# Gated attention with both heads of a pair in one 128-row operand

## Chip, cores and metric

One core of one Trainium2 chip. The metric is the device time of one execution in microseconds (us); runs of a kernel are compared by their median.

## What is computed

One layer of a decoder on 1024 tokens of width 1024, in float32. Only the two parts that the change touches are shown whole; `h` is the normalized input times `w_in`, cut into column groups.

```python
# group A: gated linear attention, 4 heads, dk = 64, dv = 128, low-rank gate of 16 columns
log_a = log_sigmoid(glr @ w_alpha2 + b_alpha) / 16
b     = cumsum(log_a) within a chunk;  qe = q * exp(b);  ke = k * exp(-b)
A     = where(causal, qe @ ke.T, 0)
o     = A @ v + qe @ S_prev              # S: the running 64 x 128 state of a head
S     = S * exp(b_last) + (k * exp(b_last - b)).T @ v
o     = rms_norm(o) * silu(gr)
# group B: sliding-window softmax attention, 8 query heads on 2 key heads of 64
...
x = x + concat(o_A, o_B) @ w_out
x = x + (silu(a) * b) @ w_down           # [a, b] = causal_conv3(rms_norm(x) @ w_up)
```

The kernel takes 128 tokens at a time (8 tiles of tokens, `t` = 0 to 7), not chunks of 64: `b` is counted from the middle of the 128, so that the same formulas hold for them.

## The kernel before

The program is a list of small steps, each put down with a due time by `at(time, step, ...)`, sorted by it and issued in that order. The due times are in units of one dense block of the projection (24 matmuls). `TQ, TK, TV, TG, TR, TO = 0.0, 8.0, 12.8, 20.8, 28.8, 36.8` are the starts of the stages: query projection of group B, its keys with the low-rank gate, values of group A, its queries and keys, its output gate, and the output projection; after that come the two large matrix products of the MLP (`product` and `down_pair`). The container in which the program is built then orders each engine's instructions by a planner with a timeline of its own, so that a step's instructions can stand inside a dense block that the list has ahead of it or behind it; buffers and dependences hold either way.

Large products are split into a high and a low float32r part and take three passes each (`PASSES`); the small products of the gated attention are plain float32 and show as two records of a matmul and two weight loads each in the trace.

The steps around the change, for a tile `t`:

- `kvl_post`, `kvl_tr`, `kvl_la` (due at TK + 0.6 t, + 1.9 and + 3.1): the 16 gate columns and a column of ones are transposed into 17 rows of a PSUM bank (L352), ACT copies them to `gt` (L362, one buffer), and the matmul L368 multiplies these 17 rows by `wa`, 16 rows of `w_alpha2` and one of `b_alpha`. ACT and DVE turn the result `za` into `la`.
- `gla_exp` (L457 to L482): running sums of `la` by matmuls with a triangle (`bd`), exponentials on ACT, and the decays `dec`.
- `gla_qk`, `gla_tr`: queries and keys are scaled from the bank of the dense block and transposed, four transposes into one bank (L498). One ACT copy (L500) takes the bank to `gqt`: two column blocks of queries, two of keys, each with the two heads of a pair in rows 0 to 63 and 64 to 127.
- `gla_state`: `cs`, the state's update, by four matmuls of 64 columns (L508), added to `state` on DVE. `gla_mid` (L523): ACT scales the four heads of the state, 64 rows each, into the two diagonal blocks of `s_mid`, whose other blocks stay zero.
- `gla_a` (due at TG + t + 1.9): the scores `ga`. For each half of the rows (`lo`) two matmuls that contract over 64 rows (L532), in a bank of their own, and a masked copy (L534, DVE) into `asb`.
- `gla_o` (due at TG + t + 2.7): four matmuls of the scores with the values (L543), and, but for the first tile, two with 256 columns of queries against the diagonal `s_mid` (L546), in the same bank. ACT and DVE then take squares, sums and a copy.
- `gate` and `gate_tr`: output gate and transposes `ogt` for the output projection.

Beside these run the steps of group B (`swa_qt`, `swa_scores`, `swa_pt`, `swa_pv`: tiles `qpt`, `sc`, `ppt`, `pv`) and the dense blocks `dk`, `dv`, `dg`, `dr`, `do` (L283, 24 matmuls each).

Banks of PSUM come from two pools of four, taken in turn (`bank`). `k2_tile` takes one of four buffers of 128 x 512.

Of the kernel before, what the change touches and what calls it, by code (L numbers as in the profile page):

```python
# [9 lines left out]
F32 = mybir.dt.float32  # L10
F32R = mybir.dt.float32r
I32 = mybir.dt.int32
AF = mybir.ActivationFunctionType
# [4 lines left out]
P = 128  # L18
# [12 lines left out]
HALF = (slice(0, 64), slice(64, 128))  # L31
# [3 lines left out]
def hymba_layer_kernel(ctx, tc, x, mix_norm, w_in, w_alpha2, b_alpha, gla_norm,  # L35
# [3 lines left out]
    act, dve, pool, pe, sp = nc.scalar, nc.vector, nc.gpsimd, nc.tensor, nc.sync  # L39
# [15 lines left out]
    def bank(name):  # L55
        ps["n"] += 1
        if "f" in ps:
            return ps["f"][2 + ps["n"] % 2]

        for start, which in (("n2pt_6", "b"), ("do1_7", "a"), ("n2pt_3", "a")):  # L60
            if name.startswith(start):
                return ps[which].tile([P, 512], F32, tag="b", name=name)
        return ps["ab"[ps["n"] % 2]].tile([P, 512], F32, tag="b", name=name)
# [40 lines left out]
    gl = sg.enter_context(tc.tile_pool(name="gl", bufs=1))  # L104
# [10 lines left out]
    amask = gl.tile([P, P], I32, name="amask")  # L115
# [40 lines left out]
    def rms_scale(ss, n, w, name, p, tag, bufs=3):  # L156
        v = p.tile([P, w], F32, tag=tag + "v", name=name + "v", bufs=bufs)
        dve.tensor_scalar(v, ss, 1.0 / n, EPS, op0=ALU.mult, op1=ALU.add)
        r = p.tile([P, w], F32, tag=tag + "r", name=name + "r", bufs=bufs)
        pool.tensor_tensor(r, v, mhalf[:, :w], ALU.pow)  # L160
        return r
# [128 lines left out]
    kt = gl.tile([P, 2, T + P], F32R, name="kt")  # L290
# [4 lines left out]
    sinks_s = gl.tile([P, 8], F32, name="sinks_s")  # L295
    qkn = gl.tile([P, 2], F32, name="qkn")
    wqk = gl.tile([P, 1], F32, name="wqk")
    wa = gl.tile([17, 256], F32, name="wa")
    glan = gl.tile([P, 1], F32, name="glan")

    def load_small():
# [10 lines left out]
    def k2_tile(name):  # L312
        return gl.tile([P, 512], F32, tag="k2", name=name, bufs=K2)
# [19 lines left out]
    kvl = {}  # L333
# [14 lines left out]
    def kvl_tr(t):  # L348
        kn, gn = kvl[t]
        pt = bank(f"kpt{t}")  # L350
        pe.transpose(pt[:, 0:P], kn, ident)
        pe.transpose(pt[0:17, P:2 * P], gn, ident)  # L352
        c = (t + 1) * P
        kl = gl.tile([P, P], F32R, tag="kl", name=f"kl{t}", bufs=2)
        for g in range(2):
            r, o = HALF[g], HALF[1 - g]
            act.activation(kt[r, g, c:c + P], pt[r, 0:P], AF.Copy, scale=wqk[r])
            dve.scalar_tensor_tensor(kl[r], pt[r, 0:P], wqk[r], kt[r, g, c:c + P].bitcast(F32),
                                     op0=ALU.mult, op1=ALU.subtract)
            act.dma_start(kt[o, g, c:c + P].bitcast(F32), kl[r].bitcast(F32))  # L360
        gt = gl.tile([17, P], F32, tag="gt", name=f"gt{t}", bufs=1)
        act.copy(gt, pt[0:17, P:2 * P])  # L362
        kvl[t] = gt

    def kvl_la(t):
        gt = kvl[t]
        pt = bank(f"za{t}")
        pe.matmul(pt[:, 0:256], lhsT=gt, rhs=wa, start=True, stop=True)  # L368
        z = pt[:, 0:256]
        e = k2_tile(f"lae{t}")[:, 0:256]  # L370
        act.activation(e, z, AF.Abs)
        act.activation(e, e, AF.Exp, scale=-1.0)
        act.activation(e, e, AF.Ln, bias=1.0)
        dve.scalar_tensor_tensor(la[:, t, :], z, 0.0, e, op0=ALU.min, op1=ALU.subtract)
# [72 lines left out]

    state = gl.tile([P, 2, P], F32, name="state")  # L450
    s_mid = [gl.tile([P, 2, 256], F32, name=f"s_mid{i}") for i in range(2)]
    asb = [gl.tile([P, 2, 256], F32, name="asb0")]
    for s in s_mid + asb:
        pool.memset(s, 0.0)
    gkd, gdec, gex, gqk, gqt, glh, grs, vg = {}, {}, {}, {}, {}, {}, {}, [None]

# [37 lines left out]
    def gla_tr(t):  # L494
        qk = gqk[t]
        pb = bank(f"gt{t}")
        for i in range(4):
            pe.transpose(pb[:, i * P:(i + 1) * P], qk[:, i * P:(i + 1) * P], ident)  # L498
        qt = k2_tile(f"gqt{t}").rearrange("p (i c) -> p i c", i=4)
        act.copy(qt, pb.rearrange("p (i c) -> p i c", i=4))  # L500
        gqt[t] = qt

    def gla_state(t):
        kd, v, dc = gkd[t], vg[0][:, t, :], gdec[t]
# [12 lines left out]

    def gla_mid(t):
        dc, sm = gdec[t], s_mid[t % 2]
        for h in range(4):  # L520
            pr, lo = h // 2, h % 2
            r = HALF[lo]
            act.activation(sm[r, pr, lo * P:(lo + 1) * P], state[r, pr], AF.Copy,  # L523
                           scale=dc[r, pr * 2:pr * 2 + 1])

    def gla_a(t):
        qt = gqt[t]
        for lo in range(2):
            pb = bank(f"ga{t}_{lo}")
            r = slice(lo * 64, (lo + 1) * 64)  # L530
            for pr in range(2):
                pe.matmul(pb[:, pr * P:(pr + 1) * P], lhsT=qt[r, 2 + pr, :], rhs=qt[r, pr, :],  # L532
                          start=True, stop=True)
            dve.copy_predicated(asb[0][:, lo].rearrange("p (q c) -> p q c", q=2),  # L534
                                amask.rearrange("p (q c) -> p q c", q=1).broadcast_to((P, 2, P)),
                                pb[:, 0:256].rearrange("p (q c) -> p q c", q=2))

    def gla_o(t):
        qt, a, v = gqt[t], asb[0], vg[0][:, t, :]
        pb = bank(f"go{t}")  # L540
        for h in range(4):
            pr, lo = h // 2, h % 2
            pe.matmul(pb[:, h * P:(h + 1) * P], lhsT=a[:, lo, pr * P:(pr + 1) * P],  # L543
                      rhs=v[:, h * P:(h + 1) * P], start=(h == 0), stop=(t == 0 and h == 3))
        for pr in range(2 if t else 0):
            pe.matmul(pb[:, pr * 256:(pr + 1) * 256], lhsT=qt[:, pr, :], rhs=s_mid[t % 2][:, pr, :],  # L546
                      start=False, stop=(pr == 1))
        sq = k2_tile(f"gsq{t}")
        act.activation(sq, pb, AF.Square)
        ss = gl.tile([P, 4], F32, tag="gss", name=f"gss{t}", bufs=2)  # L550
        dve.tensor_reduce(ss, sq.rearrange("p (h d) -> p h d", d=P), op=ALU.add, axis=AX.X)
        dve.tensor_copy(v, pb)
        grs[t] = rms_scale(ss, P, 4, f"g{t}", gl, "gr", 8)
# [438 lines left out]
    def at(time, f, *a):  # L992
        ev.append((time, len(ev), f, a))
# [7 lines left out]
    for c in halves:  # L1001
        pb = bank(f"mix{len(mix_ps)}")
# [7 lines left out]
    TQ, TK, TV, TG, TR, TO = 0.0, 8.0, 12.8, 20.8, 28.8, 36.8  # L1010
# [23 lines left out]
    for t in range(NT):  # L1034
        if t > 1:
            if t > 2:
                at(t - 2.7, load_x, t)
                at(t - 2.5, norm1_stat, t)
            if t > 2:
                at(t - 1.6, norm1_tr, t)  # L1040
            at(TQ + t, unit_q, t)
        at(TK + 0.6 * t, unit_k, t)
        at(TK + 0.6 * t + 1.9, kvl_tr, t)
        at(TK + 0.6 * t + 3.1, kvl_la, t)
        at(TV + t, unit_v, t)
        at(TG + t, unit_g, t)
        at(TR + t, unit_r, t)
        at(TO + t, unit_o, t, 0)
        u = TO + 8 + (2 * t if t < 4 else 2 * t - 7)
        at(u, unit_o, t, 1)  # L1050
        at(u + 0.005, norm2_rows, t)
        if t < 7:
            at(u + 1.9, norm2_tr, t)
        if 4 <= t < 7:
            at(u + SUMS, norm2_sums, t)
# [15 lines left out]
    for t in range(NT):  # L1071
        s = 11.0 + 1.9 * t
        at(s - 0.3, swa_qt, t)
        at(s + 1.0, swa_scores, t, 0)
        at(s + 1.6, swa_scores, t, 1)
        at(s + 3.2, swa_pt, t, 0)
        at(s + 3.8, swa_pt, t, 1)
        at(s + 4.9, swa_pv, t)
        s = TG + t
        at(s - 2.4, gla_lh, t)  # L1080
        at(s - 1.4, gla_exp, t)
        at(s + 1.0, gla_tr, t)
        if t < NT - 1:
            at(s + 1.8, gla_state, t)
            at(s + 1.85, gla_mid, t + 1)
        at(s + 1.9, gla_a, t)
        at(s + 2.7, gla_o, t)
        at(TR + t + 1.3, lambda tt=t: gate_tr(tt, psb.pop(("r", tt))))
# [113 lines left out]
```

## Time and profile before

| | |
|---|---|
| median of 3 runs | 1078.79 us (1077.31 to 1079.29) |
| profiled execution | 1077.32 us, span 1075.5 us |
| TensorE (PE) busy | 1061.8 us, 99% |
| weight loads (PEld) busy | 854.0 us, 79% |
| VectorE (DVE), ScalarE (ACT), GpSimd (POOL) busy | 785.0, 493.9, 635.6 us |
| data moved | 67.13 MB, 62 GB/s in the mean |
| granted TensorE clock | 1.0 |

Times in the profile are microseconds from the span's start. A line such as L532 is a line of the kernel before. Matmul starts are recorded and their ends modelled, so rows of neighbouring groups overlap by a few tenths in the timeline; the chain that ended last gives each group only the time by which it moved the end.

### The profile page before, as it was taken

How to read it: one execution, taken by the hardware profiler on the slowest of the kernel's cores; microseconds unless marked ns; L12 is line 12 of the kernel's file. 1: busy time of each engine (PE TensorE's matmuls, PEld its weight loads, DVE VectorE, ACT ScalarE, POOL GpSimd, SP SyncE). 2: the span in 40 equal slices, each digit the busy share in tenths (PEclk: the TensorE clock that was granted, in tenths of full speed). 3: DMA queues.
4: the chain of work that ended last, by engine and by line, in shares of the span. 5: the costliest groups of instructions: out<-in, count | busy, mean ns of one | idle time of the engine just before them, and what ended most of it. 6: DMA issues, size and time to landing. Idle time of an engine off the chain costs nothing.

```text
span 1075.5 us, 13899 instructions
## 1 busy us (share of the span) xinstructions
PE 1061.8 (99%) x4976; PEld 854.0 (79%) x4976; DVE 785.0 (73%) x1287; ACT 493.9 (46%) x998; POOL 635.6 (59%) x509
## 2 busy tenths in 40 slices
PE   7999999999999999999999999999999999999998
PEld 5898778777788878788888888888888888888886
DVE  6665546555122279888988979797979799897976
ACT  5326646546231235554444444444444445444441
POOL 4392224234552323856878787777868697877750
PEclk9999999999999999999999999999999999999999
DMA  6152113102007201121111111212121111111104
GB/s 214 54 146 62 34 30 99 33 6 69 11 25 250 59 1 39 60 59 48 51 41 58 59 59 43 76 40 79 39 62 38 59 40 59 59 59 59 40 20 157
DMA packets 67342, 67.13 MB, mean 62 GB/s; under 512 B 4616, under 2 KB 51913, under 8 KB 67274
## 3 DMA queue, kind: packets, MB, share of 16 engines
q1 hardware_dynamic: 63432, 61.53, 18.4%
q10 hardware_dynamic: 3842, 4.73, 1.9%
q8 instruction: 39, 0.64, 0.2%
q14 instruction: 29, 0.24, 0.1%
HBM read 57.33 MB, written 4.19 MB: 57 GB/s over the span
## 4 chain that ended last, share of the span: by engine, by line
PE 96%; DMA 1%; DVE 1%; ACT 1%; issue 0%; POOL 0%; SPq 0%; DVEq 0%; ACTq 0%
PE fb L775 38%; PE dn_P L956 18%; PE do L283 7%; PE dg L283 4%; PE dv L283 4%; PE dr L283 4%; PE dq L283 3%; PE dk L283 2%; PE pv L444 1%; PE ppt L432 1%; PE dq L649 1%; PE gb L775 1%; PE fb L983 1%; PE dl L983 1%; PE sc L400 1%; PE ga L532 1%
## 5 line engine op out<-in xcount | busy, mean ns | idle before, releaser
L956 PE MATMUL dn_P<-dw,dg 128*128 128x512 f32 x840 | 215.6, 392 | 0.0
L960 DVE TENSOR_TENSOR acc<-acc,dn_P 128x1024 f32<-128x1024 f32 x140 | 169.9, 1214 | 62.5 <-PE dn_P L956 62.3
L956 PEld LDWEIGHTS dn_P<-dw,dg 128*128 128x128 f32 x840 | 157.7, 188 | 37.1
L283 PE MATMUL do<-wow,big 128*128 128x512 f32 x384 | 92.9, 398 | 0.0
L95 POOL TENSOR_TENSOR dw<-dn,dw 128x512 fp32r<-128x512 f32 x50 | 69.9, 1398 | 27.4 <-PE dn_P L956 22.3
L283 PEld LDWEIGHTS do<-wow,big 128*128 128x128 f32 x384 | 71.1, 188 | 16.3
L827 ACT COPY ca<-fb 128x512 f32<-128x512 f32 x62 | 36.3, 585 | 72.2 <-PE fb L775 72.1
L421 POOL TENSOR_TENSOR pr<-pr,sm 128x1024 f32<-128x1024 f32 (+1 forms) x16 | 28.6, 1787 | 63.9 <-DVE sm L419 45.6
L775 PE MATMUL fb<-big,S1w 128*128 128x512 f32 x252 | 62.9, 396 | 0.0
L775 PE MATMUL fb<-big,A11w 128*128 128x512 f32 x252 | 62.9, 396 | 0.0
L775 PE MATMUL fb<-ex,S2w 128*128 128x512 f32 x252 | 62.8, 397 | 0.0
L775 PE MATMUL fb<-big,S4w 128*128 128x512 f32 x252 | 62.7, 396 | 0.0
L775 PE MATMUL fb<-ex,S3w 128*128 128x512 f32 x252 | 62.6, 397 | 0.0
L782 DVE SCALAR_TENSOR_TENSOR ua<-fb,cc,ua 128x511 f32<-128x511 f32 x84 | 62.2, 740 | 0.6 <-ACT ua L787 0.2
L775 PE MATMUL fb<-big,A12w 128*128 128x512 f32 x252 | 62.5, 396 | 0.0
L775 PE MATMUL fb<-ex,A22w 128*128 128x512 f32 x252 | 62.5, 397 | 0.0
L775 PEld LDWEIGHTS fb<-big,S1w 128*128 128x128 f32 x252 | 47.4, 188 | 11.6
L775 PEld LDWEIGHTS fb<-big,S4w 128*128 128x128 f32 x252 | 47.4, 188 | 11.6
L775 PEld LDWEIGHTS fb<-big,A11w 128*128 128x128 f32 x252 | 47.4, 188 | 11.6
L775 PEld LDWEIGHTS fb<-ex,S3w 128*128 128x128 f32 x252 | 47.3, 188 | 11.6 <-POOL S3w L95 0.3
L775 PEld LDWEIGHTS fb<-ex,A22w 128*128 128x128 f32 x252 | 47.4, 188 | 11.4
L775 PEld LDWEIGHTS fb<-ex,S2w 128*128 128x128 f32 x252 | 47.4, 188 | 11.4
(433 smaller groups left out, 2442.4 us busy)
## 6 DMA issues: line engine op xcount, KB each, us to landing
up<-in_w_up_dram SPq DMA_DIRECT2D x44, 512.0 KB, 3.8
dn<-in_w_down_dram SPq DMA_DIRECT2D x22, 512.0 KB, 3.5
acc<-in_x_dram SPq DMA_DIRECT2D x8, 512.0 KB, 6.9
out_dram<-acc SPq DMA_DIRECT2D x16, 256.0 KB, 2.0
xt<-in_x_dram SPq DMA_DIRECT2D x7, 512.0 KB, 3.9
qraw<-in_w_in_dram SPq DMA_DIRECT2D x4, 512.0 KB, 7.4
vraw<-in_w_in_dram SPq DMA_DIRECT2D x4, 512.0 KB, 4.1
graw<-in_w_in_dram SPq DMA_DIRECT2D x4, 512.0 KB, 3.5
```

Of the source, the lines that this page charges most:

```text
L95: (eng or pool).tensor_sub(lo, src, hi.bitcast(F32))
L283: pe.matmul(pb[:, :n], lhsT=big[:, t, k, ra, :], rhs=ws[k][:, rb, :n], start=(k == 0 and i == 0), stop=(k == KD - 1 and i == 2))
L400: pe.matmul(pbs[-1][:, j % 2, :], lhsT=q[:, g, qc], rhs=kt[:, g, kc], start=True, stop=False)
L421: pool.tensor_tensor(pr[:, :, s0:], pr[:, :, s0:], den[:, hs].rearrange("p (j o) -> p j o", o=1).broadcast_to((P, 4, n)), ALU.mult)
L432: pe.transpose(pb[:, j * P:(j + 1) * P], pr[:, j, b * P:(b + 1) * P], ident)
L444: pe.matmul(pb[g * 64:(g + 1) * 64, :], lhsT=vv[:, t - 1 + b, g * 64:(g + 1) * 64], rhs=pts[t, g][:, b, :], start=(b == b0), stop=(b == 1))
L775: pe.matmul(pb, lhsT=w[:, ra, k, :], rhs=b_operand(bn, k, rb), start=(onto is None and i == 0), stop=(i == 11), skip_group_check=onto is n ...
L782: dve.scalar_tensor_tensor(dst, src, w, dst, op0=ALU.mult, op1=ALU.add)
L827: act.copy(dst, pb)
L956: pe.matmul(pb[:, i], lhsT=g[:, ra, c:c + P], rhs=w[:, rb, :], start=(onto is None and n == 0), stop=(n == 2), skip_group_check=onto is no ...
L960: dve.tensor_add(acc, acc, pb)
L983: pe.matmul(pb, lhsT=g[:, ra, (t % 4) * P:(t % 4 + 1) * P], rhs=w[:, rb, :], start=(ch == NCH - 2 and i == 0), stop=(ch == NCH - 1 and i = ...
```

## The change

- **Gate.** `wa` and `gt` become full 128-row tiles that are zeroed once; the gate's 17 rows are copied into rows 0 to 16 of the one `gt`, and the matmul for `za` contracts over 128 rows. `kvl_la` is due at + 2.4 in place of + 3.1.
- **Queries.** The transposed queries go into `qbd[t % 2]`, for each pair of heads a 128 x 256 operand with one head in the upper left block and the other in the lower right one; the rest is zeroed once. Two ACT copies of 64 rows fill the diagonals, a third takes the keys to `gkt`.
- **Scores.** Two matmuls of 128 rows and 256 columns into one bank in place of four of 64 rows in two banks, and one masked copy of 128 x 512 in place of two of 128 x 256.
- **State.** `s_mid` is no longer diagonal: 128 x 128 a pair, scaled by two ACT instructions of 128 rows in place of four of 64.
- **Output.** The product with the state takes four matmuls of 128 columns (weights from `qbd`) in place of two of 256.

```diff
-    wa = gl.tile([17, 256], F32, name="wa")
+    wa = gl.tile([P, 256], F32, name="wa")
+    gt = gl.tile([P, P], F32, name="gt")
+    for s in (wa, gt):
+        pool.memset(s, 0.0)
...
-        gt = gl.tile([17, P], F32, tag="gt", name=f"gt{t}", bufs=1)
-        act.copy(gt, pt[0:17, P:2 * P])
-        kvl[t] = gt
+        act.copy(gt[0:17], pt[0:17, P:2 * P])
...
-    s_mid = [gl.tile([P, 2, 256], F32, name=f"s_mid{i}") for i in range(2)]
-    asb = [gl.tile([P, 2, 256], F32, name="asb0")]
-    for s in s_mid + asb:
+    s_mid = [gl.tile([P, 2, P], F32, name=f"s_mid{i}") for i in range(2)]
+    qbd = [gl.tile([P, 2, 2, P], F32, name=f"qbd{i}") for i in range(2)]
+    asb = gl.tile([P, 4, P], F32, name="asb")
+    for s in qbd + [asb]:
         pool.memset(s, 0.0)
...
-        qt = k2_tile(f"gqt{t}").rearrange("p (i c) -> p i c", i=4)
-        act.copy(qt, pb.rearrange("p (i c) -> p i c", i=4))
-        gqt[t] = qt
+        pv = pb.rearrange("p (i c) -> p i c", i=4)
+        for lo in range(2):
+            act.copy(qbd[t % 2][HALF[lo], :, lo, :], pv[HALF[lo], 0:2])
+        kt = k2_tile(f"gkt{t}")[:, 0:256].rearrange("p (i c) -> p i c", i=2)
+        act.copy(kt, pv[:, 2:4])
+        gqt[t] = kt
...
-        for h in range(4):
-            pr, lo = h // 2, h % 2
-            r = HALF[lo]
-            act.activation(sm[r, pr, lo * P:(lo + 1) * P], state[r, pr], AF.Copy,
-                           scale=dc[r, pr * 2:pr * 2 + 1])
+        for pr in range(2):
+            act.activation(sm[:, pr], state[:, pr], AF.Copy, scale=dc[:, pr * 2:pr * 2 + 1])
...
-        for lo in range(2):
-            pb = bank(f"ga{t}_{lo}")
-            r = slice(lo * 64, (lo + 1) * 64)
-            for pr in range(2):
-                pe.matmul(pb[:, pr * P:(pr + 1) * P], lhsT=qt[r, 2 + pr, :], rhs=qt[r, pr, :],
-                          start=True, stop=True)
-            dve.copy_predicated(asb[0][:, lo].rearrange("p (q c) -> p q c", q=2),
-                                amask.rearrange("p (q c) -> p q c", q=1).broadcast_to((P, 2, P)),
-                                pb[:, 0:256].rearrange("p (q c) -> p q c", q=2))
+        pb = bank(f"ga{t}")
+        for pr in range(2):
+            pe.matmul(pb[:, pr * 256:(pr + 1) * 256], lhsT=gqt[t][:, pr, :], rhs=qbd[t % 2][:, pr],
+                      start=(pr == 0), stop=(pr == 1))
+        dve.copy_predicated(asb, amask.rearrange("p (q c) -> p q c", q=1).broadcast_to((P, 4, P)),
+                            pb.rearrange("p (q c) -> p q c", q=4))
...
-        for pr in range(2 if t else 0):
-            pe.matmul(pb[:, pr * 256:(pr + 1) * 256], lhsT=qt[:, pr, :], rhs=s_mid[t % 2][:, pr, :],
-                      start=False, stop=(pr == 1))
+        for h in range(4 if t else 0):
+            pe.matmul(pb[:, h * P:(h + 1) * P], lhsT=qbd[t % 2][:, h // 2, h % 2, :], rhs=s_mid[t % 2][:, h // 2, :],
+                      start=False, stop=(h == 3))
...
-        at(TK + 0.6 * t + 3.1, kvl_la, t)
+        at(TK + 0.6 * t + 2.4, kvl_la, t)
```

More of the change, by code (lines that the diff above doesn't have):

```diff
@@ L360, in kvl_tr @@
             act.dma_start(kt[o, g, c:c + P].bitcast(F32), kl[r].bitcast(F32))
-        gt = gl.tile([17, P], F32, tag="gt", name=f"gt{t}", bufs=1)
-        act.copy(gt, pt[0:17, P:2 * P])
-        kvl[t] = gt
+        act.copy(gt[0:17], pt[0:17, P:2 * P])
     def kvl_la(t):
-        gt = kvl[t]
         pt = bank(f"za{t}")
@@ L519, in gla_mid @@
         dc, sm = gdec[t], s_mid[t % 2]
-        for h in range(4):
-            pr, lo = h // 2, h % 2
-            r = HALF[lo]
-            act.activation(sm[r, pr, lo * P:(lo + 1) * P], state[r, pr], AF.Copy,
-                           scale=dc[r, pr * 2:pr * 2 + 1])
-    def gla_a(t):
-        qt = gqt[t]
-        for lo in range(2):
-            pb = bank(f"ga{t}_{lo}")
-            r = slice(lo * 64, (lo + 1) * 64)
-            for pr in range(2):
-                pe.matmul(pb[:, pr * P:(pr + 1) * P], lhsT=qt[r, 2 + pr, :], rhs=qt[r, pr, :],
-                          start=True, stop=True)
-            dve.copy_predicated(asb[0][:, lo].rearrange("p (q c) -> p q c", q=2),
-                                amask.rearrange("p (q c) -> p q c", q=1).broadcast_to((P, 2, P)),
-                                pb[:, 0:256].rearrange("p (q c) -> p q c", q=2))
+        for pr in range(2):
+            act.activation(sm[:, pr], state[:, pr], AF.Copy, scale=dc[:, pr * 2:pr * 2 + 1])
+    def gla_a(t):
+        pb = bank(f"ga{t}")
[4 more added lines that the diff above has]
+                            pb.rearrange("p (q c) -> p q c", q=4))
     def gla_o(t):
-        qt, a, v = gqt[t], asb[0], vg[0][:, t, :]
+        v = vg[0][:, t, :]
         pb = bank(f"go{t}")
         for h in range(4):
-            pr, lo = h // 2, h % 2
-            pe.matmul(pb[:, h * P:(h + 1) * P], lhsT=a[:, lo, pr * P:(pr + 1) * P],
-                      rhs=v[:, h * P:(h + 1) * P], start=(h == 0), stop=(t == 0 and h == 3))
-        for pr in range(2 if t else 0):
-            pe.matmul(pb[:, pr * 256:(pr + 1) * 256], lhsT=qt[:, pr, :], rhs=s_mid[t % 2][:, pr, :],
-                      start=False, stop=(pr == 1))
+            pe.matmul(pb[:, h * P:(h + 1) * P], lhsT=asb[:, h, :], rhs=v[:, h * P:(h + 1) * P],
+                      start=(h == 0), stop=(t == 0 and h == 3))
+        for h in range(4 if t else 0):
+            pe.matmul(pb[:, h * P:(h + 1) * P], lhsT=qbd[t % 2][:, h // 2, h % 2, :], rhs=s_mid[t % 2][:, h // 2, :],
+                      start=False, stop=(h == 3))
         sq = k2_tile(f"gsq{t}")
```

## Prediction

> **What bounds the kernel now.** I read the page first, then the busy time by stretch, then the chain of work that ended last, then the timeline of the engines that feed TensorE. The page's share of the chain by engine:
>
> ```profile
> PE 96%; DMA 1%; DVE 1%; ACT 1%; issue 0%; POOL 0%; SPq 0%; DVEq 0%; ACTq 0%
> ```
>
> The two stretches that hold the change (busy time of each engine, clock last but two): the keys, the gate and the values, and then the gated attention.
>
> ```profile
> 54.00:160.00 106.00, 106.00 (x607) 86.14 (x606) 59.14 (x201) 55.54 (x178) 45.31 (x47) 1.00 0.26 69
> 160.00:290.00 130.00, 130.00 (x771) 103.16 (x770) 67.47 (x194) 69.41 (x188) 52.05 (x41) 1.00 0.17 46
> ```
>
> TensorE has no idle time in 236 us there, and DVE, ACT and POOL are busy about half of it. So a TensorE instruction that goes away, or gets shorter, is worth its share of the chain, and the other engines' instructions are worth nothing as long as they come in time. From the chain, in order of time (start, us, what):
>
> ```profile
> 80.41 3.01 PE dk L283 x24
> 83.64 0.62 PE za L368 x2
> 84.26 3.20 PE dk L283 x24
> ...
> 188.72 1.26 PE ga L532 x8
> 189.98 5.79 PE dg L283 x24
> ...
> 202.16 0.59 PE cs L508 x8
> 202.74 5.57 PE dg L283 x23
> ...
> 285.75 5.60 PE dr L283 x24
> ```
>
> What to see: a group that uses only part of the array's rows is dear twice, once in its own length and once in the next one's. A block of 24 with 512 columns takes 5.60 us (285.75), but 5.79 right behind a `ga` group; `dk` takes 3.20 behind `za` and 3.01 elsewhere. So the exit from the 64-row or 17-row group costs 0.19. The column group `cs` has the same exit: 23 matmuls at 202.74 take 5.57, where 23/24 of 5.60 is 5.37.
>
> **Gate: 17 rows to 128.** One `za` costs 0.62 + 0.19 = 0.81. Of 128 rows the two records of 256 columns are half of the group at 213.89 in the next fence (four records, 0.86): 0.43, and no exit. Ends: 0.22 (the smallest pair of float32 records I see, of 128 columns, a quarter of 0.89 at 212.99) and the old 0.81, if the length has another cause than the rows; I take 0.43, the row of the same shape and type. The group view counts the instances, and the chain has the groups of the scores and of the output:
>
> ```profile
> L368 PE MATMUL za<-wa,gt 17*128 17x256 f32 x16 | 5.6, 426 | 0.0
> ```
>
> ```profile
> L532 PE MATMUL ga<-gqt 64*128 64x128 f32 x64 | 9.2, 297 | 0.0
> ...
> L534 DVE COPY_PREDICATED asb<-amask,ga 128x256 f32<-128x256 int32 x16 | 6.9, 446 | 11.7 <-PE ga L532 10.8 <-PE go L543 0.8
> ```
>
> ```profile
> 200.93 0.64 PE ga L532 x4
> ...
> 212.99 0.89 PE go L543 x8
> 213.89 0.86 PE go L546 x4
> ...
> 244.19 0.64 PE ga L532 x4
> ...
> 256.30 0.65 PE ga L532 x8
> ...
> 265.82 0.59 PE cs L508 x8
> 266.41 0.65 PE ga L532 x8
> ...
> 277.11 0.65 PE ga L532 x8
> ```
>
> Sixteen records are eight `za`: 8 x (0.81 - 0.43) = **3.0 us less**. The columns that move stay 256.
>
> **Scores: four matmuls of 64 rows to two of 128.** The 64 records of `ga` lie in 12 groups: one of eight records with 1.26 (188.72), eight of four with 0.64 (200.93 the first, 244.19 the last: tiles 1 to 4, each half by itself), three of eight with 0.65 (256.30 the first, 277.11 the last). With an exit each: 1.26 + 8 x 0.64 + 3 x 0.65 + 12 x 0.19 = 10.6 us. After: eight groups of four records of 128x256, 8 x 0.86 = 6.9. Five of the old groups stand right behind `cs` (188.72 the first, 266.41 the last); there the switch from `cs` is paid now in `ga`'s own length and then by the 128-row group as an exit from `cs`: 5 x 0.19 = 0.95 more. 10.6 - 7.8 = **2.8 us less**. It is not alike everywhere: a tile whose halves stand apart pays 2 x 0.83 now and 0.86 after; the three tiles of 0.65 pay 0.84 now and 0.86 to 1.05 after. Ends for one new group: 0.64, the length of a 64-row group, and 1.24 with an entry and an exit that other neighbours make (0.86 + 2 x 0.19); 0.86 is the row of the same shape.
>
> The Trainium skill's page "TensorE: Matmul & The Clock Gate", Part 3, Packing small matmuls, speaks against this part: matmuls on different row groups run at the same time, so that filling the array's rows gives a saving away. The trace agrees in three tiles of eight (eight records in 0.65 us) and not in the other five.
>
> **Output.** The product with the state: two matmuls of 256 columns, four records, 0.86 (213.89), become four of 128, eight records like `go`'s 0.89 at 212.99. 7 x 0.03 = **0.2 us more** (tile 0 has none). Ends 0 and 7 x 0.2, if the more numerous weight loads delay anything.
>
> **Off TensorE.** The rows that price it:
>
> ```profile
> 0.98 0.31 POOL L292 MEMSET kt<- 128x256 f32 x1
> ...
> 5.63 0.55 POOL L160 TENSOR_TENSOR n10r<-n10v,mhalf 128x1 f32<-128x1 f32 x1 [2.25 <-DVE n10v L158]
> ...
> 81.18 0.24 ACT L362 COPY gt<-kpt 17x128 f32<-17x128 f32 x1
> ...
> 196.93 0.38 ACT L471 ACTIVATE ex<-bd 128x256 f32<-128x256 f32 x1
> 197.21 0.38 ACT L472 ACTIVATE ex<-bd 128x256 f32<-128x256 f32 x1
> ...
> 264.66 0.58 ACT L500 COPY gqt<-gt 128x512 f32<-128x512 f32 x1
> ...
> 267.12 1.64 ACT L523 ACTIVATE s_mid<-state,dec 64x128 f32<-64x128 f32 x4
> ```
>
> Two more memsets, of at most 0.31 each, fit into POOL's 2.25 us of idle time before its first need (those of `qbd` take the place of `s_mid`'s); `wa`'s DMAs come after them. The copy from the transposes' bank, 0.58, becomes three of 256 columns, which start 0.28 apart like L471 and L472: 0.94, so `ga`'s operands come 0.36 later (ends: 0.24 each, the smallest copy, and 0.58 each, 1.2 later). In tile 6 the copy ended at 265.24 and `ga` began at 266.41: 1.2 us of cover, the least that I saw; if it were gone, the step would cost 0.4 us a tile, 2.9 in all. `s_mid` takes half of its 1.64, and the masked copies go from 2 x 0.446 to between 0.45 and 0.89 for one of twice the width: both gains, or nothing, for engines that wait anyway. The new wait is the copy into `qbd`, which needs `gla_o` of two tiles before to be read out: for the copy at 264.66 that product was over ahead of the `ga` at 256.30, 8 us before, so the wait is over when it begins; else ACT's copies of `ppt` and `go` would queue behind it, and `ga` and TensorE behind these. The scores take one bank for two; no wait for a bank shows here. `kvl_la` moves up by 0.7 of a block; `gt` has one buffer before and after, so `za` of a tile still precedes the next copy.
>
> **Sum.** 3.0 + 2.8 - 0.2 = 5.6 us. The profiled execution took 1077.32 (span 1075.5); it would be 1071.7. It lies 1.5 below the median of the runs shown; from 1078.79 the sum gives **1073.2**. A change is told from none here at about 0.2%, 2.2 us. What is late next is TensorE itself; I look for the gain to arrive, since the chain holds TensorE through the projections behind this stage, and its later steps off TensorE start from TensorE's end:
>
> ```profile
> 330.57 33.87 PE do L283 x145
> 364.43 0.02 issue
> ...
> 380.66 0.63 PE n2pt L238 x4
> ```
>
> **Rivals.**
> - *Switches stay.* The new order puts all eight score groups between column groups (`cs`, `pv`), so that each pays entry and exit: 1.24, 9.9 us in all, and the scores give 0.7. With the gate, 3.0 + 0.7 - 0.2 = 3.5: 1075.3. For it: five groups already stand behind `cs`. Against: what follows most of them is a dense block.
> - *The halves overlap anyway.* If all eight tiles ran like the three of 0.65, the scores would cost 8 x 0.84 = 6.7 before and 7.8 after, 1.1 lost: 3.0 - 1.1 - 0.2 = 1.7 less, 1077.1. Against it are the eight groups of 0.64. By the rule of the Trainium skill cited above this is the case to expect; the trace bears it out for three tiles.
> - *Given back at a later wait.* The planner orders everything anew; where TensorE waits after the stage (before 380.66, for the first normalized rows) the steps on ACT, DVE and POOL come no earlier and over 3.4 of the 5.6 us go: 1076.6 to 1078.8, no change that can be told. Against: that chain starts from TensorE at 364.43.
> - *Slower: `za` ahead of its operand.* Its due time comes earlier, behind fewer dense matmuls; ACT's copy to `gt` began at 81.18, while `za` came at 83.64, 2.2 us after the copy's end: that is all its cover, less than the 3.01 of one dense block. If the planner's order puts `za` in front of a late copy, TensorE stands, and the dense block behind it with it. From a mean wait of 1.0 us for each of the eight it takes more than the 5.6 and 2.2 back; at 1.5 us the time is 1085.2. Against: the planner already puts a `za` in the middle of a dense block, which the list issues whole, so it seems to wait until it holds the operand for ready:
>
> ```profile
> 111.86 2.57 PE dv L283 x11
> 114.43 0.62 PE za L368 x2
> 115.05 3.22 PE dv L283 x13
> ```
>
> **Chances.** The sum as worked out 0.66; switches stay 0.10; halves overlap 0.04; given back 0.12; slower 0.08. Faster by over 0.2%: 0.66 + 0.10 = 0.76; within 0.2%: 0.04 + 0.12 = 0.16; slower 0.08. The range: below, all pairs apart (10.6 - 6.9 = 3.7), the gate and no cost of the output, 6.7, the scatter of the runs, 1.5 below the median, and about 1 for a luckier order: 1069.5. Above, it takes in the first two rivals and most of the third: 1078.0. All ends of the prices on one side would give 0.7 us more (no gain at the gate, 0.7 at the scores, 1.4 lost at the output), on the other 4.7 + 5.5 = 10.2 less; neither is likely to meet in every term.
>
> **What would show it.** Right: `za` and `ga` with 128 rows, `ga` 32 records in eight groups of about 0.86 in the chain, the group behind `za` at its bare length, no idle time of TensorE from 54 to 290, and the dense blocks after the stage 5 to 6 us earlier, kept to the end. Wrong: exits of 0.19 that are still there, waits of TensorE for `gt`, `qbd` or `gkt`, or a wait behind 360 that has grown by what the stage gained.

## Result and the profile after

| | before | after |
|---|---|---|
| median | 1079.04 us, 4 runs (1077.31 to 1079.34) | 1086.96 us, 4 runs (1085.49 to 1090.5) |
| profiled execution, span | 1075.5 us | 1085.4 us |
| ratio | | 1.0089, 95% interval 1.0074 to 1.0104 |

Medians are of all executions; ratios leave out three that ran far longer than the rest of their kernel: 1164.65 us with the due time at + 2.45 (whose median is 1082.68 without it), 2126.25 with the scores alone and 3708.13 in the last experiment.

The change made the kernel 0.9% slower, where 0.5% faster was forecast. The chain of the changed kernel is still TensorE's. As the experiments show, the gate's term of the sum is there in full and the scores' in part; what was costed at nothing, the earlier `za`, took nearly three times as much away. The busy time by stretch (same columns as before):

```profile
54.00:160.00 106.00, 97.86 (x552) 82.89 (x551) 52.95 (x180) 46.78 (x149) 40.88 (x45) 0.94 0.24 64
160.00:290.00 130.00, 130.00 (x765) 103.65 (x764) 69.57 (x202) 72.00 (x212) 50.16 (x38) 1.00 0.19 50
```

TensorE now has 8.1 us of idle time in the first stretch, and a granted clock of 0.94 in place of 1.00. The second stretch has neither. Who waited for whom, TensorE's rows:

```profile
PE za L368 <- ACT gt L364: 4.5, 2, 3.6
...
PE sc L400 <- DMA qt<-qt: 3.1, 1, 3.1
...
PE sc L401 <- DMA ql<-ql: 0.5, 1, 0.5
```

4.5 + 3.1 + 0.5 is the whole of it. The chain shows both places:

```profile
79.18 3.01 PE dk L283 x24
82.19 0.45 PE za L368 x2
...
82.66 0.24 ACT lae L371
...
83.39 0.36 ACT kt L360
83.75 0.32 ACT lae L372
...
84.09 0.42 ACT lae L373
...
85.19 0.37 DVE kl L361
...
85.58 0.47 ACTq L363
...
86.09 0.26 ACT gt L364
...
86.40 1.22 PE za L368 x2
88.05 5.06 PE dk L283 x24
...
104.22 0.45 PE za L368 x2
...
112.13 1.22 PE za L368 x2
113.35 7.03 PE dv L283 x24
```

Read it downwards: a `za` ends at 82.64, and the next `za` needs `gt`. On ACT the copy to `gt` is the last of its step and stands behind the first `za`'s own three activations, the copies to `kt`, the DVE subtraction between them and the issue of a DMA; TensorE waits 3.6 us. TensorE's own timeline shows why nothing covers this:

```profile
82.02 0.59 PE L368 MATMUL za<-wa,gt 128*128 128x256 f32 x2
82.46 0.27 PE L354 MATMUL kpt<-ident,kn 128*128 128x128 f32 x1
82.56 0.27 PE L355 MATMUL kpt<-ident,gn 128*17 128x128 f32 x1
86.40 1.22 PE L368 MATMUL za<-wa,gt 128*128 128x256 f32 x2 [3.57 <-ACT gt L364]
```

The second `za` stands right behind the transposes (`kpt`) that its copy reads. They end at 82.83, and the copy starts 3.3 us later. In the kernel before, the first copy starts 3.0 us behind its transposes too,

```profile
77.96 0.27 PE L352 MATMUL kpt<-ident,gn 128*17 128x128 f32 x1
```

that is, at 81.18; but there a dense block and a half and the transposes of two more tiles lie between these transposes and their `za` at 83.64. At the second place the first scores of a tile come behind the transposes of its queries (`qpt`, 104.96) with only two small transposes and a `za` between, so the cast and the DMA of the queries (issued at 106.91) are waited for until 109.33, and then `gt` for 0.9 us more; with both parts and the late `za`, further down, two `dv` blocks lie between (93.54 to 106.49). Why the planner chose that order is not shown.

TensorE pays again: the granted clock falls, and a `dk` block takes 5.06 us in place of 3.01, a `dv` block 7.03 in place of 5.60. Four windows of 4 us (granted clock third from the end) show it:

```profile
84.00:88.00 4.00, 1.60 (x5) 1.25 (x6) 1.11 (x4) 1.43 (x6) 0.65 (x1) 0.71 0.20 49
88.00:92.00 4.00, 4.00 (x20) 4.00 (x19) 1.84 (x7) 2.07 (x8) 0.80 (x2) 0.50 0.06 16
...
108.00:112.00 4.00, 1.34 (x4) 0.90 (x4) 2.49 (x8) 3.04 (x10) 1.04 (x1) 0.70 0.52 130
112.00:116.00 4.00, 3.87 (x9) 3.11 (x10) 1.27 (x5) 1.79 (x6) 0.79 (x3) 0.50 0.21 51
```

### The profile page after: what moved, and what is told of

Same layout as the page of the kernel before. It is cut to its first block, busy times and chain, and to the rows that moved or that the text cites. A ratio compares the mean times of both kernels' runs of the same rounds, so it can differ in the third digit from the quotient of the medians.

```text
span 1085.4 us, 13897 instructions
## 1 busy us (share of the span) xinstructions
PE 1064.9 (98%) x4972; PEld 860.6 (79%) x4972; DVE 783.6 (72%) x1279; ACT 491.1 (45%) x1000; POOL 636.4 (59%) x511
## 4 chain that ended last, share of the span: by engine, by line
PE 95%; DVE 1%; DMA 1%; ACT 1%; POOL 0%; issue 0%; ACTq 0%; SPq 0%
PE fb L772 38%; PE dn_P L953 18%; PE do L283 7%; PE dv L283 4%; PE dg L283 4%; PE dr L283 4%; PE dq L283 3%; PE dk L283 2%; PE pv L444 2%; PE ppt L432 1%; PE dq L646 1%; PE gb L772 1%; PE fb L980 1%; PE dl L980 1%; PE go L540 1%; PE sc L400 1%
```

## Experiments

The theory after this reading: both operands of 128 rows are worth what they were costed at or near it, and the loss is only the place of `za`, 0.7 of a block earlier in the list, ahead of a late copy. The rivals: the single `gt` tile written in place; the 128 rows themselves; the diagonal blocks, by another order of everything.

For the comparison of stages I use the chains of the profiles, since the first 80 us differ by up to 3 us between the profiled executions: from the start of the `dk` block ahead of the first `za` (80.41 before, 79.18 after) to the first transposes of the second norm (380.66 before, 390.48 after). That is 300.25 us before and 311.30 after.

**Each part alone.** First the scores without the gate:

```diff
 # from the changed kernel
-    wa = gl.tile([P, 256], F32, name="wa")
-    gt = gl.tile([P, P], F32, name="gt")
...
+    wa = gl.tile([17, 256], F32, name="wa")
...
-        act.copy(gt[0:17], pt[0:17, P:2 * P])
+        gt = gl.tile([17, P], F32, tag="gt", name=f"gt{t}", bufs=1)
+        act.copy(gt, pt[0:17, P:2 * P])
...
-        at(TK + 0.6 * t + 2.4, kvl_la, t)
+        at(TK + 0.6 * t + 3.1, kvl_la, t)
```

> The queries as diagonal blocks, the scores, the state and the output as changed; the gate as before (17 rows, due at +3.1). Theory (the loss is all in the gate's stage, where za was moved ahead of its operand): no idle time of TensorE from 80 to 125 us, and the scores give what the stage behind 160 us shows in the changed kernel, 1.4 us less than before: 1077.6. Rival (the diagonal blocks shift the planner's order everywhere and that is what costs): slower than before by several us, with waits for gt or for the queries' DMAs although the gate is untouched.

1076.75 us, ratio 0.998 (0.9972 to 0.9989). No wait in the stage; the stretch is 298.78 us (81.24 to 380.02), 1.5 less. Then the gate without the scores:

> The gate as changed (128 rows, one gt, due at +2.4); the scores as before. Theory: the whole loss is here: waits of TensorE for gt of 4 to 5 us and the slower clock behind them; 10 us or more over before, about 1089. Rival (it takes both parts): within 2 us of before.

1089.88 us, 1.0105 (1.0091 to 1.0118), with the same waits, 4.5 us for `gt` and 3.1 for the queries' DMA. So the loss is all in the gate. Its due time alone, in the kernel before:

```diff
-        at(TK + 0.6 * t + 3.1, kvl_la, t)
+        at(TK + 0.6 * t + 2.4, kvl_la, t)
```

> The kernel before with nothing changed but the due time of kvl_la, +2.4 in place of +3.1. Theory (the place of za in the order is the cause): the same waits for gt as in the changed kernel, 10 us or more slower than before, about 1090. Rival (the fixed gt tile, written in place, or the 128 rows, bring the waits): the time of before, 1079, within 2 us.

1093.4 us, 1.0134 (1.0118 to 1.015): one number makes the kernel before slower than the whole change does. Its waits of TensorE:

```profile
PE za L368 <- ACT gt L362: 4.3, 2, 3.4
...
PE sc L400 <- DMA qt<-qt: 2.5, 1, 2.5
```

And the 128 rows without the due time:

```diff
 # from the kernel before
-    wa = gl.tile([17, 256], F32, name="wa")
+    wa = gl.tile([P, 256], F32, name="wa")
+    gts = [gl.tile([P, P], F32, name=f"gt{i}") for i in range(3)]     # all zeroed once
...
-        act.copy(gt, pt[0:17, P:2 * P])
+        act.copy(gts[t % 3][0:17], pt[0:17, P:2 * P])
```

> The gate with 128 rows but at its old due time, +3.1, which takes three zeroed gt tiles in turn; the scores as before. Theory (rows good, place bad): no wait for gt, za 0.43 us each with no slower matmul behind: 8 x 0.38 = 3.0 us less than before, 1076. Rival (the rows or the planner's cost for them are at fault): as slow as the changed kernel, 1087.

1074.24 us, 0.9965 (0.9951 to 0.9978). Its chain, beside the rows of before at 80.41 to 84.26:

```profile
80.26 3.01 PE dk L283 x24
83.49 0.43 PE za L369 x2
83.92 3.00 PE dk L283 x24
...
155.65 5.79 PE dv L283 x24
```

`za` takes 0.43 as costed, and the block behind it 3.00 in place of 3.20. From the `dk` block to the last `dv` block it is 75.39 us here and 78.35 before (80.41 to 158.76): 2.96 less, where 3.0 was forecast.

**The two parts together, without the due time.**

```diff
 # from the changed kernel
-    gt = gl.tile([P, P], F32, name="gt")
+    gts = [gl.tile([P, P], F32, name=f"gt{i}") for i in range(3)]
...
-        at(TK + 0.6 * t + 2.4, kvl_la, t)
+        at(TK + 0.6 * t + 3.1, kvl_la, t)
```

> The whole change, with kvl_la at its old due time, +3.1, and three zeroed gt tiles in turn for it. Theory: the two parts add up, -2.2 (scores only) and -3.8 (128-row gate at the old time) from 1079: about 1073, no wait of TensorE between 54 and 300 us. Rival (the parts disturb each other's order): near 1076 or above.

1074.02 us, 0.9965 (0.9954 to 0.9977). By the stretch of the chain the parts add up: 295.73 us (80.83 to 376.56), 4.5 less than before, where the scores alone give 1.5 and the gate alone 3.1. The medians do not add up so: 2.3 and 4.8 for the parts, 4.0 for both. They mix in a clock that falls at a later place, shown further down: it fell in 12 of the 18 executions of before beside the parts, in 3 of 10 and 2 of 7 of theirs, and then in 7 of 14 of before beside this kernel and 5 of its own 7 (a mean clock of 0.998). Among the executions with a mean clock of 1.0 alone, the means are 0.6, 3.1 and 3.2 us less than before, the last from two executions; that the parts add up is shown by the stretch only.

**What makes the early `za` late.** Three kernels: one more dense block as cover, more `gt` tiles, an earlier copy.

```diff
-        at(TK + 0.6 * t + 2.4, kvl_la, t)
+        at(TK + 0.6 * t + 2.45, kvl_la, t)
```

> The whole change with kvl_la due at +2.45 in place of +2.4. In the list that puts the za of tiles 0 to 2 behind one dense block more (at +2.4 they tie with that block and go first). Theory a (the missing cover of one dense block of 3.0 us is the cause): no wait of 3 us for gt, 1073 to 1076. Theory b (with one gt tile and the copy late on ACT, any place before +2.5 stalls): 1085 or more.

1083.76 us, 1.0047 (1.0031 to 1.0063): half of the loss against before goes, and the waits for the queries' DMAs with it, but three waits for `gt` remain in the profiled execution, which at 1086.18 is the slowest of the five in the ratio (us in total, times, the longest):

```profile
PE za L368 <- ACT gt L364: 6.0, 3, 3.6
```

A block of cover is not enough; theory b stands, in a milder size than I gave it.

```diff
 # from the changed kernel, due at + 2.4
-    gt = gl.tile([P, P], F32, name="gt")
+    gts = [gl.tile([P, P], F32, name=f"gt{i}") for i in range(3)]
...
-        act.copy(gt[0:17], pt[0:17, P:2 * P])
+        act.copy(gts[t % 3][0:17], pt[0:17, P:2 * P])
...
```

> The whole change at +2.4, with three gt tiles in turn, so that no copy waits for an earlier za. Theory (the place of za alone): the waits for gt stay, 1085 to 1090. Rival (the single tile is what holds the copy back): no waits, about 1073.

1086.97 us, 1.0091 (1.0076 to 1.0105), the changed kernel's ratio (1.0089) within the intervals, with 4.9 us of waits for `gt`. The single tile is not the cause.

```diff
     def kvl_tr(t):
...
         pe.transpose(pt[0:17, P:2 * P], gn, ident)
+        act.copy(gt[0:17], pt[0:17, P:2 * P])
         c = (t + 1) * P
...
             act.dma_start(kt[o, g, c:c + P].bitcast(F32), kl[r].bitcast(F32))
-        act.copy(gt[0:17], pt[0:17, P:2 * P])
```

> The whole change at +2.4 with one gt tile, but the step kvl_tr issues the copy to gt first, ahead of the two copies to kt with their DVE subtractions and DMA issues. Theory a (za waits because ACT has kt, kl and the DMA issues, some 3 us, ahead of the copy): no wait for gt over 0.5 us, 1073 to 1077. Theory b (the early za itself disturbs the order): still over 1083, with the waits of the scores for the queries' DMAs.

1074.48 us, 0.9968 (0.9957 to 0.998). With one line moved to the front of its step, at the same early due time and with the one tile, no wait for `gt` is left in TensorE's rows, only 1.1 us for one DMA of the queries:

```profile
PE sc L401 <- DMA ql<-ql: 1.1, 1, 1.1
```

So it takes both to lose: a `za` that the list calls early, and a copy that the list puts last on ACT. How the edit helps is less plain, since the planner's order changed with it. For the same tile as at 86.40 above, ACT's row first:

```profile
80.89 0.26 ACT L356 COPY gt<-kpt 17x128 f32<-17x128 f32 x1
```

```profile
80.03 0.27 PE L355 MATMUL kpt<-ident,gn 128*17 128x128 f32 x1
80.06 3.27 PE L283 MATMUL dk<-kw,big 128*128 128x272 f32 x24
83.17 0.59 PE L368 MATMUL za<-wa,gt 128*128 128x256 f32 x2
```

The copy now starts 0.6 us behind its transposes in place of 3.3, and TensorE also has a dense block between the transposes and `za`, which it had not. Right behind its transposes, `za` would have waited about 0.9 us (an estimate from these rows: 80.30 to 81.15). The two gains were not separated.

**Why the scores gave 1.4 and not 2.6.** In the kernel with the scores alone `pv` of one more tile is cut in two by a group of `sc`; before, that tile's group is whole (224.53, 1.87):

```profile
222.72 1.00 PE pv L444 x2
...
224.39 1.86 PE pv L444 x6
```

That is 1.0 us of the missing 1.2. In the same kernel `go` stands behind `dec` and takes 1.00 (here and twice later), where it took 0.89 behind `bd` at 212.99 before:

```profile
198.06 0.34 PE dec L480 x4
198.40 1.00 PE go L540 x8
```

I moved the due time of `swa_pv` ahead of the scores', in the best kernel and in the one before:

```diff
-        at(s + 4.9, swa_pv, t)
+        at(s + 4.75, swa_pv, t)
```

> The whole change with kvl_la at +3.1 and three gt tiles, and in addition swa_pv due at s + 4.75 in place of s + 4.9, so that it comes ahead of the scores of two tiles later (due at s + 4.8). Theory (the scores' gain is short of 2.6 us because the new order splits the matmuls of one more tile's pv, 1.00 + 1.86 in place of 1.87, around a group of sc): no split group of pv in the chain, the two of the kernel without this edit gone, 2.0 us less than with kvl_la at +3.1 alone, about 1072. Rival (the split groups cost nothing, since sc runs beside them, or splits come elsewhere): 1074, no difference.

> The kernel before with nothing changed but swa_pv due at s + 4.75. Theory: its one split group (154.98 and 156.90 us) closes, 1.0 us less, 1077 to 1078. Rival: no difference, 1078 to 1079.

1073.83 us, 0.9957 (0.9944 to 0.9969), and 1077.8 us, 0.9995 (0.9986 to 1.0005). The rival holds: the groups at that place close, and other groups split, earlier in the kernel (rows of the best kernel with the edit; the one before with it has splits like these from 119.91 to 140.21):

```profile
114.38 1.00 PE pv L445 x2
120.58 1.00 PE pv L445 x2
132.85 1.00 PE pv L445 x2
134.40 1.86 PE pv L445 x6
```

By the stretch of the chain the edit brings nothing in the best kernel (78.66 to 374.64, 295.98 us, beside 295.73) and costs 0.85 in the one before (81.60 to 382.70, 301.10 us, beside 300.25). That 1077.8 lies where the theory had it is luck: the later fall of the clock came in none of its ten executions in the ratio, and in at least 10 of the 15 of before beside it. That a split costs 1.0 us is read from the rows; that its removal gives 1.0 us back was not shown. 1073.83 is the fastest of all kernels here, but no faster than the others near 1074 by more than their intervals.

## Why the prediction was wrong, point by point

- **What bounds it.** Right: TensorE's time is the kernel's time, and what it gained or lost in these stages arrived at the end. From the first `n2pt` to the end it is 694.8 to 695.1 us in six of the twelve profiles and 696.5 to 696.7 in the other six, those in which the clock falls there.
- **Gate, 3.0 us.** Right: 2.96 in the kernel that has it alone at the old due time, with the parts as costed, 0.43 for a `za` and no exit of 0.19 behind it.
- **Scores, 2.8 less 0.2.** The direction was right, the size not: the stage from the last `dv` block to the second group `ogt` is 132.59 us before (158.76 to 291.35) and 131.22 with the scores alone (159.59 to 290.81), 1.37 less. It is the same in other pairs: 132.6 with the gate alone at either due time, 131.2 in the changed kernel and with both parts and the late `za`. The groups `ga` are as costed, 0.86 or, behind `cs`, 1.06; the terms that I left out are the split `pv`, 1.0, and `go`'s entry behind `dec`, 0.11 each time, three times there and once before. The sum held each group's neighbours fixed, and the planner gave them new ones.
- **Off TensorE.** The three copies of `gla_tr` and the rest cost nothing, as said: no wait in the second stretch. But "`kvl_la` moves up by 0.7 of a block" was costed at nothing, and this is the step that failed. The cover was quoted, 2.2 us between copy and `za`, less than the 3.0 us of one dense block; the sum should have begun from there. What the cover has to hold is the time from the transposes to the copy, 3.0 us before and 3.3 after, and the new order left nothing there.
- **The rival that came true** was the one at 0.08, with its mechanism and its place. That its time (1085.2) is near is luck: it had eight waits of 1.5 us, and there are two for `gt`, 4.5 us in all, and other terms that it did not have. What I held against it was the `za` inside a dense block, from which I took it that the planner waits until its own timeline has the operand ready. That timeline is on no record; if it works so, it has the operand earlier than ACT does, since the trace has the chain `lae`, `kt`, `kl`, DMA issue, `gt` that the order made no room for. And the price missed the queries' DMA and the clock: of the 15.6 us between the early and the late `za` (90.98 us from 79.18 to 170.16, beside 75.39), 8.1 are waits, about 5.7 the half clock behind them (an estimate: half of the 11.5 us that TensorE was busy at 0.50, by windows of 1 us), and 1.0 is one more split `pv` (136.90 and 138.27).
- **Given back at a later wait.** Not so: from the second `ogt` group to the first `n2pt` it is 89.3 us before (291.35 to 380.66), 89.1 after (301.38 to 390.48) and 89.2 with both parts and the late `za` (287.41 to 376.56); only a clock that falls behind that point, below, takes something back in some executions.

## What to carry to other kernels

A moved step is costed by what its first instruction reads: follow the copy that feeds it back through its engine's queue, DMA issues and all, and set that beside the cover that the old place gave. Where the trace shows a producer later than a planner's order has its consumer, put the producer earlier in its own step, which here was worth 12 us, with the new order that it brought. When a change has a good part and an incidental one, as a due time that a single buffer asks for, try the good part without it (here two more small tiles).

## What was not expected of the hardware

An idle TensorE paid twice here. Behind waits of 3.6 and 3.1 us the granted clock was 0.50 for several us. But a shorter wait was followed by the same: ahead of the first `n2pt` TensorE waits 2.0 to 2.3 us in every kernel here, and the 14 matmuls behind it take 3.27 us in the profile of before,

```profile
381.28 3.27 PE do L283 x14
```

and 4.80 in the kernel with both parts and the late `za`:

```profile
376.56 0.63 PE n2pt L238 x4
377.19 4.80 PE do L283 x14
```

The mean granted clock of whole executions shows that it comes and goes: the kernel before ran at 1.0 in 6 of 18 runs beside the first four experiments (1076.5 to 1077.5 us) and at 0.998 in 12 (1078.1 to 1080.2). The profiles fit: 3.26 or 3.27 us for the 14 in those with a mean clock of 1.0, 4.4 to 4.8 in the three at 0.998. By the two groups of profiles above, the fall costs 1.6 us. So a part of each ratio above is the share of executions that were hit. The Trainium skill's page "TensorE: Matmul & The Clock Gate", Part 1, has the array go to half its clock after an idle window of about 3.4 us, in a window that runs freely; the trace agrees on the half and on the chance in it, but here 2.0 us of waiting came before the fall in some executions.
